# A hybrid recurrent layer on one core: a pinned pair of expansions, and column sums by products of 512 columns

## The chip, the core and the metric

The kernel runs on one core of a Trainium2 chip. TensorE multiplies matrices, VectorE, ScalarE and GpSimd work on tiles in SBUF, and each engine, with SyncE, can issue transfers on its queue. The metric is the time of one execution in device microseconds, the median over several runs.

## The reference

One layer of a streaming encoder is computed for a prompt of 512 frames and a sample of 64, with 2048 features, all in fp32:

```
mod = silu(c) @ w_ada + b_ada;  sh1, sc1, g1, sh2, sc2, g2 = split(mod, 6)
h = rmsnorm(x, norm1) * (1 + sc1) + sh1
proj = h @ w_in                     # gated linear attention (4 heads), gated delta rule (8 heads)
mix = concat(gla(...), gdn(...)) @ w_out
x = x + g1 * mix
h = rmsnorm(x, norm2) * (1 + sc2) + sh2
gate, val = split(h @ w_up, 2)
x = x + g2 * ((silu(conv3(gate) + b) * val) @ w_down)
y = rmsnorm(x, final_norm)
```

`c` is one vector for the prompt and one for the sample, `w_ada` is 2048 x 12288. The delta rule runs a causal convolution of width 4 on q, k and v, and solves, in every block of 64 frames, a unit lower triangular system:

```
lower = strict_tril(kb @ k.T * decay)
sol = triangular_solve(eye + lower, [v * beta, kb * exp(G)])
```

## The kernel before

Prompt and sample go through together, 576 columns as two halves of 288. Every large product is three fp32r products, since a weight tile is split into a high part on ScalarE (L651, `wh`) and a rest on VectorE (L652, `wl`): `hh,wh`, `hl,wh` and `hh,wl`, each for two halves, six matmuls for a step of 128 rows (`mm6`, L562 and L564). A weight tile holds 8 such steps, and `wh` and `wl` come from rings of three.

After the head come 54 column tiles of the input projection (`in_tile`, 16 steps each), then the output projection, the up and the down projection. Under the input projection run three streams, advanced a bit after each step by `tick`: the *jobs* (the recurrences, one per head, written as generators that yield and `rest` a number of ticks), `later` (a function that is to run so many ticks on), and *ada*, the modulation's remaining 16 blocks of 512 columns. The order in which instructions are then placed on an engine is chosen by the framework's scheduler from dependencies and priorities; each engine executes its list in order, so an instruction that waits holds all behind it.

*The inverse.* `inverse16` inverts the 16 x 16 diagonal blocks of a delta job. The matrices go to DRAM and come back with 32 blocks on 32 partitions (`d<-m`, `m<-d`), GpSimd works through 14 rows (L372 and L373), and the result goes to DRAM (L378) and comes back as `cm`, 128 partitions. After REST_X ticks, and 14 more (`FIRST_LATE`) in the first job, VectorE expands `cm` by a block mask into two tiles `m` of 512 columns (L387, twice). From them TensorE doubles the block size: L247, an eviction on VectorE (L1941), L254, and so on.

*The convolution.* `gdn_conv` copies a projected tile to `gcb`, and runs one product on ScalarE and three multiply-adds on VectorE (L1005).

*The modulation.* `ada_block` takes half-megabyte pieces of `w_ada` and accumulates them on VectorE, with one column of silu(c) as the scalar, into `acc` of 128 x 512 for prompt and sample (L833 starts, L835 goes on, 32 instructions a block). The sum over partitions is left: eight fp32 matmuls with `acc` as weights and a column of ones as the other side (L841) put 8 columns into PSUM, with the 512 outputs on partitions; the trace shows 16, since fp32 takes two passes. `put_mod` (L812) adds the bias from there.

Of the kernel before, what the change touches and what calls it, by code (L numbers as in the profile page):

```python
# [8 lines left out]
F32 = mybir.dt.float32  # L9
F32R = mybir.dt.float32r  # L10
I32 = mybir.dt.int32
AF = mybir.ActivationFunctionType
ALU = mybir.AluOpType
# [3 lines left out]
P = 128  # L17
# [18 lines left out]
REST_D, REST_X, REST_T, REST_N, REST_G = 8, 12, 6, 8, 4  # L36
# [8 lines left out]
FIRST_LATE = 14  # L45
# [58 lines left out]
class Kern:  # L104
# [67 lines left out]

        return cols.unsqueeze(2).to_broadcast([P, cols.shape[1], w])

    def gdn(self, qF, kF, x, gain, hcols, gb_src, s0, s_out, o_put, last_level, late=0):

# [4 lines left out]
        nc, c = self.nc, self.c  # L183
        V, A, T = self.jv, self.ja, nc.tensor
# [50 lines left out]
        u, t = yield from self.inverse16(a, gb, late)  # L235
# [5 lines left out]
        turn = lambda: None  # L241
        for s in (16, 32):
# [14 lines left out]
            if s < last_level:  # L257
                turn = lambda s=s: A.activation(half(t, s, 0), half(self.transpose4(u), s, 0), AF.Copy)
# [23 lines left out]
        for b in range(4):  # L282
# [12 lines left out]
            w = self.half()  # L295
# [54 lines left out]
    def inverse16(self, a, spare, late):  # L350

        nc, c, G = self.nc, self.c, self.nc.gpsimd
        pitch = 4 * P
        d0 = self.dp.tile([8 * (16 * pitch + 16)], F32, tag="d0", bufs=2, name=self.name("d0"))
        d1 = self.dp.tile([2, 32, 256], F32, tag="d1", bufs=2, name=self.name("d1"))
        G.dma_start(d0[:P * pitch].rearrange("(p f) -> p f", p=P), a.rearrange("p b t -> p (b t)"))
        lane = spare[:32].rearrange("p b t -> p (b t)").rearrange("p (w f) -> p w f", w=2)  # L360
        xx, xt = [lane[:, n].rearrange("p (i j) -> p i j", i=16) for n in range(2)]
        yield from self.rest(REST_S)
        blocks = d0.rearrange("(n f) -> n f", n=8)[:, :16 * pitch].rearrange("n (i b j) -> n i b j", i=16, b=4)
        for b in range(4):
            G.dma_start(xx[8 * b:8 * b + 8], blocks[:, :, b, :16])
        yield from self.rest(REST_D)
        G.memset(lane[:, 0, 0:256:17], 1.0)
        for i in range(1, 15):
            yield WAIT
            rest = slice(i + 1, 16)  # L370
            sh = [32, 15 - i, i]
            G.tensor_tensor(xt[:, rest, :i], xx[:, rest, i:i + 1].to_broadcast(sh), xx[:, i:i + 1, :i].to_broadcast(sh), op=ALU.mult)  # L372
            G.tensor_tensor(xx[:, rest, :i], xx[:, rest, :i], xt[:, rest, :i], op=ALU.add)  # L373
            yield WAIT
        yield from self.rest(REST_P)
        G.tensor_copy(xt, xx.rearrange("p i j -> p j i"))
        yield from self.rest(2)
        G.dma_start(d1.rearrange("w q f -> q w f"), lane)  # L378
        yield from self.rest(REST_S)
        cm = self.sp.tile([P, 2, 4, 16], F32, tag="cm", bufs=2, name=self.name("cm"))  # L380
        for w in range(2):
            G.dma_start(cm[:, w], d1[w].rearrange("(b n) (i j) -> (n i) b j", b=4, i=16))
        yield from self.rest(REST_X + late)
        sh = [P, 4, 8, 16]
        t, u = self.m4(), self.m4()
        for w, x in enumerate((t, u)):
            nc.vector.tensor_tensor(x.rearrange("p b (n j) -> p b n j", n=8), cm[:, w].unsqueeze(2).to_broadcast(sh),  # L387
                                    c["bd16"].rearrange("p (n j) -> p n j", n=8).unsqueeze(1).to_broadcast(sh), op=ALU.mult)
        yield from self.rest(HOP)
        return u, t  # L390

# [430 lines left out]
    def ada_block(self, blk, acc, raw):  # L822

        nc = self.nc
        V, T = nc.vector, nc.tensor
        acc = [a() for a in acc]
        for k0 in range(0, KD, 2):
            w = raw(blk, k0)
            for k in range(2):
                for s in range(2):  # L830
                    col = self.ct[:, s, k0 + k:k0 + k + 1]
                    if k0 + k == 0:
                        V.tensor_scalar_mul(acc[s], w[:, k], col)  # L833
                    else:
                        V.scalar_tensor_tensor(acc[s], w[:, k], col, acc[s], op0=ALU.mult, op1=ALU.add)  # L835
                    yield
        yield from self.rest(4)
        pc = self.bank()
        for j in range(4):
            for s in range(2):  # L840
                T.matmul(pc[:, 2 * j + s:2 * j + s + 1], acc[s][:, j * P:(j + 1) * P], self.c["ones"][:, 0:1],  # L841
                         start=True, stop=True)
        self.put_mod(blk // 4, 4 * (blk % 4), pc)

    def ada_raw(self, blk, k0):

# [147 lines left out]
    def gdn_conv(self, ps, t, dst, name, h):  # L994

        nc = self.nc
        V, A = nc.vector, nc.scalar
        cb = self.gcb
        acc = self.ap.tile([P, 582], F32, tag="ca", bufs=1, name=self.name("ca"))
        A.activation(cb[:, 3:515].rearrange("p (h t) -> p h t", h=2), ps[:, :, :HP], AF.Copy)  # L1000
        V.tensor_copy(cb[:, 518:582].rearrange("p (h t) -> p h t", h=2), ps[:, :, HP:HT])
        A.activation(cb[:, 515:518], self.vmap["st_conv"].rearrange("p (i t) -> p t i", i=3)[:, t], AF.Copy)
        A.activation(acc[:, :579], cb[:, 0:579], AF.Copy, scale=self.vec("gdn_conv_w", t))
        for j in range(1, 4):
            V.scalar_tensor_tensor(acc[:, :579], cb[:, j:j + 579], self.vec("gdn_conv_w", 24 * j + t), acc[:, :579],  # L1005
                                   op0=ALU.mult, op1=ALU.add)
        A.activation(dst, acc[:, 0:512], AF.Silu)
        A.activation(self.cs[:, 0, :, t], cb[:, 512:515], AF.Copy)
        A.activation(self.cs[:, 1, :, t], cb[:, 579:582], AF.Copy)
        self.put_s(name, h, lambda s: A.activation(s, acc[:, 515:579], AF.Silu))  # L1010
# [13 lines left out]
    def gdn_heads(self):  # L1024
        nc, o = self.nc, self.o
        A = nc.scalar
        b4 = lambda t: t.rearrange("p (b t) -> p b t", b=4)
        def conv_tile(n, off, h):
            ps = (self.ps_q0, self.ps_k0)[n] if h == 0 and n < 2 else self.in_tile(off + h * P)
            t = self.m("qkv")  # L1030
            self.gdn_conv(ps, 8 * n + h, t, "qkv"[n], h)
            return b4(t)

        def qk(h):
            q = conv_tile(0, OFF_BQ, h)
            if h == 0:
                self.narrow(self.kp)
            k, x = conv_tile(1, OFF_BK, h), {}
            self.jobs.append(self.gdn(q, k, x, self.vec("gdn_norm", 0), slice(4 * h, 4 * h + 4),
                                      self.gd[4 * h:4 * h + 4], None, o["p_gdn"][0, 0, h],  # L1040
                                      lambda t: self.put_o(8 + h, t), 64, FIRST_LATE if h == 0 else 0))
            return x

        def vg(h, x):
            v = conv_tile(2, OFF_BV, h)
            x["v"], x["at"] = lambda: v, self.ticks
            if h in GATES_BY:
                self.side = self.gla_gate(GATES_BY.index(h))
            ps = self.in_tile(OFF_BG + h * P)
            gt = self.m("gt")  # L1050
            A.activation(self.halves(gt), ps[:, :, :HP], AF.Silu)
            self.put_s("g", h, lambda t: A.activation(self.halves(t), ps[:, :, HP:HT], AF.Silu))
            x["gate"] = lambda: b4(gt)

        xs = [qk(0)]
        for h in range(8):
            if h < 7:
                xs.append(qk(h + 1))
            vg(h, xs[h])
        self.jobs.append(self.gdn_samples())  # L1060

        for s in range(2):
            ps = self.bank()
            nc.tensor.transpose(ps[:72, :P], self.cs[:, s].rearrange("p i t -> p (i t)"), self.c["ident"])
            rw = self.half()
            nc.vector.tensor_copy(rw[:72], ps[:72, :P])
            nc.sync.dma_start(o["ps"[s] + "_conv"][0, 0].rearrange("i (n p) -> i n p", p=P).rearrange("i n p -> (i n) p"), rw[:72])
# [778 lines left out]
def layer_kernel(tc, i, o):  # L1846
    nc = tc.nc
    with ExitStack() as ctx:
# [17 lines left out]
        with ExitStack() as early:  # L1866
            K.wp = pool(early, "wp", "right", bufs=3)
            with ExitStack() as right:
# [9 lines left out]
                with ExitStack() as st:  # L1878
# [3 lines left out]
                    K.jobs, K.due, K.ticks, K.at_job, K.at_ada = [], [], 0, 0.0, 0.0  # L1882
                    K.dp = dp
                    acc = [lambda n=n: K.ap.tile([P, 512], F32, tag=f"acc{n}", bufs=1, name=K.name("acc")) for n in range(2)]
                    K.ada = K.ada_blocks(range(8, 24), acc)
                    K.side = iter(())
                    K.gdn_heads()
# [10 lines left out]
                    K.drain()  # L1898
                    for _ in K.ada:
                        pass  # L1900
            K.sp = pool(ctx, "sp2", bufs=2)
            K.zp = pool(ctx, "zp", bufs=1)
            K.ua = pool(ctx, "ua", bufs=1)
# [99 lines left out]
```

## Time and profile before

| | |
|---|---|
| median of 3 runs | 2853.79 us (2853.17 to 2856.24) |
| the profiled execution | 2861.94 us, span 2860.2 us |
| mean granted TensorE clock | 0.987 |
| TensorE, VectorE, ScalarE, GpSimd busy | 2787.5, 2248.9, 1296.2, 317.9 us |
| the last L841 | begins at 1123.9 us |

Times inside the trace count from the start of the span. In a row of a timeline the brackets hold the idle time of the engine before that row and what ended it. In a row by window the engines stand in the order named in its head, then the granted clock, the DMA share and GB/s. Up to about 140 us is the head, the input projection runs to about 1085, the output projection to about 1310, the up projection to 2300, and the rest is the down projection and the end.

### The profile page before, as it was taken

The numbers are of one execution on the slowest core, as the hardware profiler recorded it, in microseconds if no ns is written. First come the engines' busy times: TensorE is split into PE (matmuls) and PEld (weight loads), VectorE is DVE, ScalarE is ACT, GpSimd is POOL, SyncE is SP. The second block draws the span as 40 slices with busy tenths as digits, with TensorE's granted clock in tenths as the row PEclk, the third lists the DMA queues.
The fourth block names the chain that finished last, engine by engine and source line by source line (L and its number), as shares of the span: only waits on it lengthen the run. The fifth ranks groups of instructions, "written<-read, shape, count | busy, mean of one in ns | idle before, by whom it ended". The sixth has DMA issues, their size and how long they took to land.

```text
span 2860.2 us, 51761 instructions
## 1 busy us (share of the span) xinstructions
PE 2787.5 (97%) x20560; PEld 2698.7 (94%) x20560; DVE 2248.9 (79%) x3728; ACT 1296.2 (45%) x2286; POOL 317.9 (11%) x597
## 2 busy tenths in 40 slices
PE   7898999999999999999999999999999999999998
PEld 3598999999999999999999999999999999999997
DVE  2477888777778787478887888888888889999996
ACT  4264556544433333255444444444444464444553
POOL 1023333224210001000000000000000000000000
PEclk9999999999999999999999999999999999999999
DMA  9964555545456448433333333333333343444461
GB/s 331 338 183 134 147 160 155 165 137 162 121 158 180 141 131 257 117 114 102 102 102 107 103 110 104 102 108 109 101 102 102 109 145 117 124 123 124 125 171 67
DMA packets 521984, 399.77 MB, mean 140 GB/s; under 512 B 50681, under 2 KB 453442, under 8 KB 521742
## 3 DMA queue, kind: packets, MB, share of 16 engines
q1 hardware_dynamic: 515966, 385.55, 45.6%
q0 software_dynamic: 5776, 10.91, 1.3%
q8 instruction: 162, 2.65, 0.4%
q14 instruction: 80, 0.66, 0.1%
HBM read 356.24 MB, written 40.13 MB: 139 GB/s over the span
## 4 chain that ended last, share of the span: by engine, by line
PE 79%; DVE 9%; issue 5%; DMA 4%; ACT 1%; POOL 1%; SPq 0%; ACTq 0%; DVEq 0%; POOLq 0%
PE g L562 19%; PE g L564 9%; PE g L1385 9%; PE g L1386 8%; PE g L1387 8%; PE bank L1386 3%; PE bank L1385 3%; PE bank L1387 3%; DVE wl L1570 2%; PE g L1618 2%; PE g L1620 2%; PE g L1619 2%; DMA raw<-in_w_down_dram 1%; DVE slot L1635 1%; PE bank L164 1%
## 5 line engine op out<-in xcount | busy, mean ns | idle before, releaser
L1385 PE MATMUL g<-slot,wh 128*128 128x290 f32 x1760 | 533.1, 303 | 2.7 <-ACT p L1397 2.7
L1386 PE MATMUL g<-slot,wh 128*128 128x290 f32 x1760 | 526.0, 299 | 0.0
L1387 PE MATMUL g<-slot,wl 128*128 128x290 f32 x1760 | 520.4, 296 | 0.0
L562 PE MATMUL g<-hh,wh 128*128 128x288 f32 x1984 | 450.1, 307 | 3.9 <-ACT wh L651 2.8
L564 PE MATMUL g<-hh,wl 128*128 128x288 f32 x1984 | 434.1, 299 | 3.5 <-DVE wl L652 3.4
L562 PE MATMUL g<-hl,wh 128*128 128x288 f32 x1984 | 432.2, 298 | 0.0
L1332 ACT ACTIVATE wh<-raw 128x1024 fp32r<-128x1024 f32 x176 | 187.1, 1063 | 392.5 <-PE g L1386 379.3
L1385 PEld LDWEIGHTS g<-slot,wh 128*128 128x128 f32 x1760 | 331.2, 188 | 16.7 <-ACT p L1397 11.7
L1387 PEld LDWEIGHTS g<-slot,wl 128*128 128x128 f32 x1760 | 336.1, 191 | 0.0
L1386 PEld LDWEIGHTS g<-slot,wh 128*128 128x128 f32 x1760 | 334.4, 190 | 0.1
L562 PEld LDWEIGHTS g<-hh,wh 128*128 128x128 f32 x1984 | 320.8, 191 | 7.7 <-ACT wh L651 3.1
L564 PEld LDWEIGHTS g<-hh,wl 128*128 128x128 f32 x1984 | 321.2, 190 | 4.2 <-DVE wl L652 4.0
L562 PEld LDWEIGHTS g<-hl,wh 128*128 128x128 f32 x1984 | 322.5, 190 | 0.1
L651 ACT ACTIVATE wh<-raw 128x1024 fp32r<-128x1024 f32 x147 | 155.7, 1061 | 287.8 <-PE g L562 262.0
L835 DVE SCALAR_TENSOR_TENSOR acc<-xr,ct,acc 128x512 f32<-128x512 f32 x322 | 231.4, 752 | 0.1
L1333 DVE TENSOR_TENSOR wl<-raw,wh 128x1024 fp32r<-128x1024 f32 x176 | 214.8, 1221 | 19.8 <-ACT wh L1332 19.7
L1618 PE MATMUL g<-slot,wh 128*128 128x288 f32 x760 | 224.4, 295 | 1.2 <-DVE slot L1635 1.2
L1620 PE MATMUL g<-slot,wl 128*128 128x288 f32 x760 | 223.9, 295 | 0.3 <-DVE wl L1570 0.3
L1619 PE MATMUL g<-slot,wh 128*128 128x288 f32 x760 | 224.2, 295 | 0.0
L652 DVE TENSOR_TENSOR wl<-raw,wh 128x1024 fp32r<-128x1024 f32 x147 | 180.0, 1225 | 49.3 <-ACT wh L651 47.8
L1386 PE MATMUL bank<-slot,wh 128*128 128x290 f32 x704 | 210.6, 299 | 0.0
L1385 PE MATMUL bank<-slot,wh 128*128 128x290 f32 x704 | 210.0, 298 | 0.0
(435 smaller groups left out, 5954.2 us busy)
## 6 DMA issues: line engine op xcount, KB each, us to landing
raw<-in_w_up_dram SPq DMA_DIRECT2D x176, 512.0 KB, 4.1
raw<-in_w_in_dram SPq DMA_DIRECT2D x108, 512.0 KB, 4.2
xr<-in_w_ada_dram SPq DMA_DIRECT2D x86, 512.0 KB, 3.8
raw<-in_w_down_dram SPq DMA_DIRECT2D x76, 512.0 KB, 3.6
ax<-in_w_ada_dram SPq DMA_DIRECT2D x42, 512.0 KB, 3.7
raw<-in_w_out_dram SPq DMA_DIRECT2D x32, 512.0 KB, 5.0
actd<-v SPq DMA_DIRECT2D x44, 256.0 KB, 4.5
hraw<-in_w_ada_dram SPq DMA_DIRECT2D x21, 512.0 KB, 8.8
```

Source lines behind the costliest of these rows:

```text
L562: T.matmul(ps[:, h if bank is None else bank, :n], wh, x[:, h, :n], start=f, stop=False)
L564: T.matmul(ps[:, h if bank is None else bank, :n], wl, ah[:, h, :n], start=False, stop=stop)
L652: nc.vector.tensor_tensor(lo[:, :n_], raw[:, :n_], hi[:, :n_].bitcast(F32), op=ALU.subtract)
L835: V.scalar_tensor_tensor(acc[s], w[:, k], col, acc[s], op0=ALU.mult, op1=ALU.add)
L1332: self.nc.scalar.activation(hi, src, AF.Copy)
L1333: self.nc.vector.tensor_tensor(lo, src, hi.bitcast(F32), op=ALU.subtract)
L1385: T.matmul(ps, wh[:, j], hi, start=(c < 3 and j == 0), stop=False, skip_group_check=True)
L1386: T.matmul(ps, wh[:, j], lo, start=False, stop=False, skip_group_check=True)
L1387: T.matmul(ps, wl[:, j], hi, start=False, stop=(j == NPAIR - 1), skip_group_check=True)
L1618: T.matmul(ps, wh[:, j, f], hi, start=(c < 3 and j == 0), stop=False, skip_group_check=True)
L1619: T.matmul(ps, wh[:, j, f], lo, start=False, stop=False, skip_group_check=True)
L1620: T.matmul(ps, wl[:, j, f], hi, start=False, stop=(j == n - 1), skip_group_check=True)
```

## The change

The expansions of the first job may be placed only behind the last convolution instruction that has been given out at that time; `issue_after` fixes an order on the engine and adds no semaphore. In the other jobs nothing is pinned. And the sums over partitions are made with `acc`, split into a high part and a rest, as the moving side, and 66 columns of ones and zeros as weights: rows 0 to 32 of the bank get the prompt's sums, 33 to 65 the sample's. Two rows are copied to SBUF, written to DRAM (`md`, two transfers on ScalarE's queue), read back six ticks later with outputs on partitions (`mc`, two transfers of 128 x 4 single elements), and added to the bias 16 ticks after that place (`put_mod`, now L813).

```diff
-        yield from self.rest(REST_X + late)
+        yield from self.rest(REST_X + (late or 0))
...
-        for w, x in enumerate((t, u)):
-            nc.vector.tensor_tensor(x.rearrange("p b (n j) -> p b n j", n=8), cm[:, w].unsqueeze(2).to_broadcast(sh),
-                                    c["bd16"].rearrange("p (n j) -> p n j", n=8).unsqueeze(1).to_broadcast(sh), op=ALU.mult)
+        with self.tc.issue_after(self.conv_of) if late is not None else ExitStack():
+            for w, x in enumerate((t, u)):
+                nc.vector.tensor_tensor(x.rearrange("p b (n j) -> p b n j", n=8), cm[:, w].unsqueeze(2).to_broadcast(sh),
+                                        c["bd16"].rearrange("p (n j) -> p n j", n=8).unsqueeze(1).to_broadcast(sh), op=ALU.mult)
...
+        A = nc.scalar
+        hi, lo = [self.wq.tile([P, 1024], F32R, tag="w" + c, bufs=3, name=self.name("w" + c))
+                  .rearrange("p (s n) -> p s n", s=2) for c in "hl"]
+        for s in range(2):
+            A.activation(hi[:, s], acc[s], AF.Copy)
+            V.tensor_tensor(lo[:, s], acc[s], hi[:, s].bitcast(F32), op=ALU.subtract)
+        yield from self.rest(3)
+        pc = self.bank()
+        for n, (x, s) in enumerate((x, s) for x in (hi, lo) for s in range(2)):
+            T.matmul(pc[:66], self.pick[:, 33 * s:33 * s + 66], x[:, s], start=(n == 0), stop=(n == 3))
+        rows = self.xr()[:, :512]
+        A.activation(rows[:66], pc[:66], AF.Copy)
+        md = self.dp.tile([2, 512], F32, tag="md", bufs=2, name=self.name("md"))
+        mc = self.ap.tile([P, 8], F32, tag="mc", bufs=1, name=self.name("mc"))
+        for s in range(2):
+            A.dma_start(md[s:s + 1], rows[33 * s:33 * s + 1])
+
+        def turn():
+            for s in range(2):
+                A.dma_start(mc[:, s:8:2], md[s].rearrange("(j p) -> p j", p=P))
+
+        self.later(6, turn)
+        self.later(16, lambda: self.put_mod(blk // 4, 4 * (blk % 4), mc))
         yield from self.rest(4)
-        pc = self.bank()
-        for j in range(4):
-            for s in range(2):
-                T.matmul(pc[:, 2 * j + s:2 * j + s + 1], acc[s][:, j * P:(j + 1) * P], self.c["ones"][:, 0:1],
-                         start=True, stop=True)
-        self.put_mod(blk // 4, 4 * (blk % 4), pc)
...
             V.scalar_tensor_tensor(acc[:, :579], cb[:, j:j + 579], self.vec("gdn_conv_w", 24 * j + t), acc[:, :579],
                                    op0=ALU.mult, op1=ALU.add)
+        self.conv_of = nc.cur_bb.bb.instructions[-1]
...
+                    K.pick = K.ap.tile([P, 99], F32R, name="pick")
+                    for n, f in enumerate((1.0, 0.0, 1.0)):
+                        nc.scalar.activation(K.pick[:, 33 * n:33 * n + 33], K.c["ones"][:, :33], AF.Copy, scale=f)
...
                     for _ in K.ada:
                         pass
+                    K.run_later(all=True)
```

`late` is now None by default and for every job but the first. A line of the new file stands one further down up to the modulation, 18 or 19 after it, and 23 for the recurrences' helper (L1941 becomes L1964). The following rows are the engines' lists as the two programs hold them.

VectorE before, at the first job's expansions; `s` and `rk` are small tiles of that job, `acc` the modulation's:

```order
255 L1941 TENSOR_TENSOR rk_2029<-nbe,s_291_1897 128x4
256 L387 TENSOR_TENSOR m_2502<-cm_2272,consts_1312 128x512
257 L1941 TENSOR_TENSOR s_291_1897<-nbeta,s_291_1897 128x4
258 L1941 TENSOR_TENSOR qkv_1583<-qkv_1583,m_1777 128x512
259 L1941 TENSOR_TENSOR m_1932<-bank_2094,m_1932 128x512
260 L387 TENSOR_TENSOR m_2503<-cm_2272,consts_1312 128x512
261 L1941 TENSOR_TENSOR m_1931<-bank_2093,m_1931 128x512
262 L812 TENSOR_TENSOR mod<-bank_2125,cols 128x8
263 L833 TENSOR_SCALAR acc_2135<-ax_1988,ct 128x512
```

VectorE now, where the expansions (L388) stand; L843 is the rest of `acc`:

```order
303 L1023 SCALAR_TENSOR_TENSOR ca_2457<-gcb,cols,ca_2457 128x579
304 L836 SCALAR_TENSOR_TENSOR acc_2192<-xr_2626,ct,acc_2192 128x512
305 L1023 SCALAR_TENSOR_TENSOR ca_2457<-gcb,cols,ca_2457 128x579 x2
306 L388 TENSOR_TENSOR m_2513<-cm_2281,consts_1312 128x512
307 L388 TENSOR_TENSOR m_2514<-cm_2281,consts_1312 128x512
308 L1964 TENSOR_TENSOR m_2596<-m_2485,cum 128x512
309 L843 TENSOR_TENSOR wl_2892<-acc_2191,wh_2891 128x512
310 L1964 TENSOR_TENSOR m_1441<-bank_2532,consts_1312 128x256
```

They moved from row 256, ahead of the second block's accumulations, to row 306 behind them; between rows 254 and 305 now lie 30 L836, 2 L834, 6 L653, 6 L1023, 2 L1019, one L813 and 6 small ones.

TensorE before, at the same job's first doubling (`m_2503` is an expansion):

```order
563 L564 MATMUL g_2461<-hh_869,wl_2464 128x288 x2
564 L247 MATMUL bank_2523<-m_2503,m_1571 128x64 x4
565 L562 MATMUL g_2461<-hh_894,wh_2463 128x288 x2
566 L562 MATMUL g_2461<-hl_895,wh_2463 128x288 x2
567 L564 MATMUL g_2461<-hh_894,wl_2464 128x288 x2
```

TensorE now:

```order
570 L565 MATMUL g_2470<-hh_1069,wl_2604 128x288 x2
571 L563 MATMUL g_2470<-hh_1094,wh_2603 128x288
572 L247 MATMUL bank_2532<-m_2514,m_1575 128x64 x4
573 L563 MATMUL g_2470<-hh_1094,wh_2603 128x288
574 L563 MATMUL g_2470<-hl_1095,wh_2603 128x288 x2
```

L247 moved from ahead of the tile's step `hh_894` into the step `hh_1094`, past the steps 894, 919, 1044 and 1069: 25 products of 288 columns on.

ScalarE now, in the third of the 16 blocks; `ca` is a gate of the linear attention, L857 the return of the sums, L652 a weight split:

```order
329 L1964 ACT_TABLE_LOAD
330 L1964 ACTIVATE ca_3766<-ca_3766,consts_95 128x512
331 L1964 ACTIVATE ca_3766<-ca_3766,consts_95 128x64
332 L857 DMA mc_3722<-md_3721 128x4x1 x2
333 L1020 ACTIVATE gcb<-cols 128x3
334 L1964 ACT_TABLE_LOAD
335 L1964 ACTIVATE m_4316<-m_4316 128x512
336 L652 ACTIVATE wh_4077<-raw_4076 128x1024
```

VectorE now, at the same block's modulation:

```order
489 L1964 TENSOR_TENSOR m_2485<-bank_3845,consts_1312 128x256
490 L1964 SCALAR_TENSOR_TENSOR ca_3766<-gcb,ca_3766 128x512
491 L1964 SCALAR_TENSOR_TENSOR ca_3766<-gcb,ca_3766 128x64
492 L1964 SCALAR_TENSOR_TENSOR gcb<-consts_95,ca_3766 128x128 x4
493 L813 TENSOR_TENSOR mod<-mc_3722,cols 128x8
494 L653 TENSOR_TENSOR wl_4078<-raw_4076,wh_4077 128x1024
```

L813 stands six instructions behind the gate that ScalarE finishes just ahead of L857; behind it waits the rest of a weight tile. The eight L841 of each block have gone from TensorE's list, and four L847 (`bank<-wh,pick` and `bank<-wl,pick`, 66x512) stand in it instead.

More of the change, by code (lines that the diff above doesn't have):

```diff
@@ L173, in col4, with gdn @@
         return cols.unsqueeze(2).to_broadcast([P, cols.shape[1], w])
-    def gdn(self, qF, kF, x, gain, hcols, gb_src, s0, s_out, o_put, last_level, late=0):
+    def gdn(self, qF, kF, x, gain, hcols, gb_src, s0, s_out, o_put, last_level, late=None):
         nc, c = self.nc, self.c
@@ L1040, in qk @@
                                       self.gd[4 * h:4 * h + 4], None, o["p_gdn"][0, 0, h],
-                                      lambda t: self.put_o(8 + h, t), 64, FIRST_LATE if h == 0 else 0))
+                                      lambda t: self.put_o(8 + h, t), 64, FIRST_LATE if h == 0 else None))
             return x
```

## The prediction

> **What bounds the kernel now.** I read the page's totals first, then busy time by stretch, then the one stretch that stands out.
>
> ```profile
> span 2860.2 us, 51761 instructions
> PE 2787.5 (97%) x20560; PEld 2698.7 (94%) x20560; DVE 2248.9 (79%) x3728; ACT 1296.2 (45%) x2286; POOL 317.9 (11%) x597
> core 0: us, PE busy (x) PEld busy (x) DVE busy (x) ACT busy (x) POOL busy (x), PEclk, DMA share, GB/s
> 200.00:310.00 110.00, 97.12 (x717) 92.94 (x716) 78.01 (x160) 48.36 (x119) 56.20 (x101) 0.94 0.46 128
> 310.00:1000.00 690.00, 688.86 (x5254) 673.19 (x5253) 541.06 (x1122) 315.30 (x736) 153.89 (x274) 0.99 0.53 154
> 1000.00:1100.00 100.00, 97.28 (x705) 92.77 (x704) 82.98 (x192) 38.59 (x72) 6.81 (x25) 0.97 0.54 155
> ```
>
> TensorE is the bound: from 310 to 1000 us it idles 1.1 us in 690, so there a microsecond taken from TensorE is a microsecond off the end, and work on VectorE (541 of 690 busy) or ScalarE (315) is free until it makes TensorE wait. From 200 to 310 us TensorE idles 12.9 us. What it idles for shows in VectorE's timeline:
>
> ```profile
> 204.35 0.16 DVE L1941 TENSOR_TENSOR rk<-nbe,s 128x4 f32<-128x4 f32 x1
> 217.78 0.69 DVE L387 TENSOR_TENSOR m<-cm,consts 128x512 f32<-128x512 f32 x1 [13.27 <-DMA cm<-d]
> 223.05 1.41 DVE L835 SCALAR_TENSOR_TENSOR acc<-xr,ct,acc 128x512 f32<-128x512 f32 x2
> 224.38 1.22 DVE L652 TENSOR_TENSOR wl<-raw,wh 128x1024 fp32r<-128x1024 f32 x1
> 238.87 0.86 DVE L1005 SCALAR_TENSOR_TENSOR ca<-gcb,cols,ca 128x579 f32<-128x579 f32 x1
> ```
>
> L387 stands at VectorE's head for 13.27 us and waits for the small inverse to come back through DRAM; the weight splits (L652) that TensorE needs are queued behind it. TensorE's own timeline, then its busy time and granted clock (the number before the DMA share):
>
> ```profile
> 221.46 0.54 PE L562 MATMUL g<-hh,wh 128*128 128x288 f32 x2 [2.85 <-ACT wh L651]
> 225.66 0.85 PE L564 MATMUL g<-hh,wl 128*128 128x288 f32 x2 [3.40 <-DVE wl L652]
> 244.85 1.00 PE L247 MATMUL bank<-m,m 128*128 128x64 f32 x8
> 252.39 1.97 PE L254 MATMUL bank<-m,m 128*128 128x64 f32 x8 [5.15 <-DVE m L1941]
> 216.00:220.00 4.00, 2.61 (x20) 2.38 (x18) 2.21 (x5) 1.42 (x5) 0.00 (x0) 1.00 0.07 9
> 220.00:225.00 5.00, 0.80 (x4) 0.57 (x4) 5.00 (x10) 3.99 (x7) 1.71 (x3) 0.84 0.31 78
> 225.00:230.00 5.00, 4.34 (x18) 4.35 (x19) 5.00 (x8) 0.00 (x0) 1.50 (x5) 0.50 0.91 264
> 245.00:250.00 5.00, 2.24 (x19) 2.01 (x17) 5.00 (x9) 1.41 (x3) 4.50 (x7) 1.00 0.86 251
> 250.00:255.00 5.00, 2.61 (x12) 2.61 (x13) 3.70 (x7) 2.57 (x5) 2.87 (x4) 0.57 0.53 152
> 255.00:260.00 5.00, 5.00 (x34) 5.00 (x34) 1.62 (x2) 0.91 (x5) 1.55 (x2) 0.75 0.70 183
> ```
>
> Idle in these rows is 1.39 + 4.20 + 0.66 + 2.76 + 2.39 = 11.4 us. Busy time at a lowered clock is lost too: 4.34 x 0.50 + 2.61 x 0.43 + 5.00 x 0.25 + 0.80 x 0.16 = 4.7 us. The stall, and the backlog behind it (the 5.15 us wait at 252), cost **16 us**.
>
> **Part one, the pin.** The two L387 instructions move from VectorE's row 256 to behind the convolution. What VectorE now runs in between, from 204.5 us: 30 accumulations (1.41/2, less overlap 0.67 each, 20.1 us), 2 starts (0.9), 6 splits (1.15 pitch, 6.9), 6 convolution steps (0.76, 4.6), and about 2.4 us of small ones: 34.9 us, to 239.4. One L813 lies among them (part two; I give it 2.7 us), and the expansions take 1.2: done at about 243.3.
>
> The late transfer `cm` is hidden: GpSimd's steps towards it slow down when VectorE is not idle,
>
> ```profile
> 203.46 0.27 POOL L373 TENSOR_TENSOR m<-m 32x44 f32<-32x44 f32 x1
> 234.75 0.71 POOL L372 TENSOR_TENSOR m<-m 32x44 f32<-32x44 f32 x1
> ```
>
> and the steps still left at 204.5 took 6.2 us; at up to 0.71/0.27 they take 16, so `cm` lands by about 228, with 13 us in hand.
>
> What is late next is TensorE's L247, which reads the expansions. It came at 244.85; without the two waits (6.25) and the half clock after them (2.2) that place is reached at 236.4. The change puts it 25 products of 288 columns later (0.134 each, row 286.72 below: 3.3), so TensorE arrives at about 239.5 and waits **about 4 us**. Another 1 us goes at L254, whose eviction stands three instructions behind the expansions on VectorE, and 2 us at a lower clock, as after the 5.15 us wait (1.1 + 1.25). Left of the 16: **9 us**. The ends: 16 if nothing waits; 3, if both later waits are twice as long and the clock drops in full.
>
> On the 2 us of clock there is also a rule: the Trainium skill ("TensorE: Matmul & The Clock Gate", Part 1) has the clock halved after an idle window of about 3.4 us that runs freely; by it a 4 us wait may or may not fill a window, and the term is 0 or 2. The row at 250 us agrees, with 5.15 us idle and 0.57 behind it.
>
> **Part two, the sums.** The old products, by source, in the chain and in place:
>
> ```profile
> L841 PE MATMUL bank<-consts,acc x256: 164/250/307, 203.9 to 1123.9; 128*128 128x1 f32 x128
> 341.63 1.68 PE bank L841 x16
> 284.62 1.90 PE L841 MATMUL bank<-consts,acc 128*128 128x1 f32 x16
> 286.72 0.43 PE L564 MATMUL g<-hh,wl 128*128 128x288 f32 x2
> 286.99 0.43 PE L562 MATMUL g<-hh,wh 128*128 128x288 f32 x2
> ```
>
> Sixteen blocks of 16 products with one column cost 1.68 us each. The four new ones are fp32r products like L562: pairs of 288 columns start 0.27 apart, so 0.134 each, and 512 columns 0.237; four take 0.95 us. Saved: 0.73 x 16 = **11.7 us** of TensorE. Were the 66 columns of weights no cheaper to load and the fill exposed (0.3, the difference between a product's duration and its pitch), 1.25 and 6.9 us.
>
> What is added, per block:
>
> ```profile
> L1000 ACT ACTIVATE gcb<-g 128x512 f32<-128x512 f32 x23 | 13.7, 596 | 3.1 <-PE g L564 3.1
> L387 DVE TENSOR_TENSOR m<-cm,consts 128x512 f32<-128x512 f32 x18 | 12.2, 688 | 13.9 <-DMA cm<-d 13.3 <-PE bank L294 0.6
> L365 POOL DMA_DIRECT2D m<-d x36 | 21.9, 614 | 23.1 <-DMA d<-m 17.9 <-DVE s L1941 2.8 <-DVE acc L835 2.4
> d<-m POOLq DMA_DIRECT2D x9, 64.0 KB, 2.0
> cm<-d POOLq DMA_DIRECT2D x18, 32.0 KB, 3.5
> ```
>
> VectorE: two subtractions, 1.4 us. ScalarE: three activations, 1.8 us, and four DMA issues on its own queue; no row shows ScalarE issuing one, so by GpSimd's 0.61 at most 2.5 us, and about 2.0 us in which the return waits for the row written out (as `d<-m`). Over 16 blocks that is 22 us on VectorE and at most 100 on ScalarE, against 149 and 375 us free from 310 to 1000. The splits queued behind the waiting ScalarE have one weight tile as cover: 8 x 6 products of 0.134, 6.4 us. The three pick activations precede the narrow phase and are lost in ScalarE's free time.
>
> The price that can hurt is L813. Before, the modulation read PSUM; now VectorE waits at its head until `mc` has come, 512 single elements. `cm<-d`, 512 pieces of 16, lands in 3.5 us. In the third block the return is issued as ScalarE finishes the gate's last activation, and on VectorE six instructions of the gate (some 1.6 us) stand between that activation and L813; so VectorE stands 3.5 + 0.8 - 1.6 = 2.7 us. Does such a stand cost TensorE? The same place has stood before, as long:
>
> ```profile
> 343.13 0.49 DVE L833 TENSOR_SCALAR acc<-xr,ct 128x512 f32<-128x512 f32 x1 [4.21 <-PE bank L841]
> 944.63 0.49 DVE L833 TENSOR_SCALAR acc<-ax,ct 128x512 f32<-128x512 f32 x1 [3.98 <-PE bank L841]
>   DVE acc L833: 22.4, 7
>   DVE mod L812: 8.8, 8
> ```
>
> VectorE waited 22.4 + 8.8 = 31 us for L841, up to 4.2 us at a time, and TensorE stayed full. Those waits go, since the accumulators are now released by the copies; 16 x 2.7 = 43 us come. I charge TensorE 0.2 us a block for it, 3 us, and 1 us for the first block, where the products follow the subtractions at once: **4 us**, bounds 0 and 12 (0.7 a block, all that the products save).
>
> The stream of blocks also ends later: its last old product stands at 1123.9, and by the order of the new program the last new ones stand at a place that was reached at 1178, with L813 at about 1184.
>
> ```profile
> 1100.00:1200.00 100.00, 98.90 (x745) 98.67 (x744) 51.34 (x78) 24.29 (x29) 4.26 (x6) 1.00 0.66 187
> L1173 DVE TENSOR_TENSOR slot<-xr,slot x4: 757/758/760, 1135.9 to 1143.1; 128x576 fp32r<-128x576 f32 x4
> ```
>
> VectorE and ScalarE are half and three quarters idle there, so the accumulations are hidden. What moves with them are four of the eight conversions of the mixers' outputs for the second half of the output projection (L1173, in the new file L1192): done by 1144 before, now behind the last block, so that all eight, 6 us, follow 1184.5. The first product that reads them stood at about 1202. I cost this at 0; were the 11 us of cover gone, it costs the length of the last L813's stand, 3 us, inside the bounds of the 4.
>
> Against `mc` speaks the Trainium skill ("DMA: Bandwidth & Descriptors", Rules for kernel authors): a last dimension that is not contiguous becomes one descriptor per element. By it `mc` has 512 descriptors, as many as `cm` has pieces, and the 3.5 us would stand; no row here has 4-byte pieces alone.
>
> **Sum.** 9 + 11.7 - 4 = 17 us off. Against the profiled execution's own 2861.9 that is 2845; its time lies 8.1 over the median 2853.8, so the median comes to **2837 us**.
>
> **Rivals.** *The stands eat the sums' gain* (0.2). For it: splits lose one of three slots in each ring while hi and lo are held. Against it: the 31 us above cost nothing. Then 11.7 goes and 9 less some 2 remains: 2847, range 2841 to 2853.
>
> *Everything is hidden* (0.1): TensorE is not late at L247 because VectorE's rows run faster than I add them, and no stand counts: 16 + 11.7 = 28 off, 2826. Against it: VectorE is 100% busy in these rows.
>
> *The wait only moves* (0.05): expansions at 243 hold TensorE, at half clock, as long as L387 did, and the sums give back all but a little: within 3 us of 2854.
>
> *Slower, by `mc`* (0.15): its pieces queue behind half-megabyte weight loads. The slowest small load has
>
> ```profile
> fr<-in_w_in_dram SPq DMA_DIRECT2D x8, 256.0 KB, 9.8
> ```
>
> and if `mc` takes 9.8, VectorE stands 9.8 - 1.6 = 8.2 us at each L813, 1.8 us beyond the cover of one tile: 16 x 1.8 = 29 lost against 21 won, 8 slower, 2862. It decides from a stand of 6.4 + 21/16 = 7.7 us. For it: the DMA share is 0.53 throughout; against: `cm` meets the same traffic and lands in 3.5.
>
> **Numbers.** The forecast has 0.5, with its own range 2830 to 2843 (terms 9 and 4 between 5 and 12, 0 and 7). A measurement of this kernel tells 0.2%, 5.7 us, from nothing: faster means under 2848, slower over 2859.5. Faster: 0.5 + 0.1 + half of the first rival, 0.70. Same: its other half and 0.05, 0.15. Slower 0.15. The range leaves out the slower case: 2825 to 2858.
>
> **What would show it.** VectorE's 13.27 us gap gone, L388 near 242 and a TensorE wait of 3 to 5 us there at L247; the windows 216 to 235 at clock 1.00; L847 four to a block in about 0.95 us; L813 waiting 1 to 4 us on DMA `mc`; TensorE still idle under 5 us from 310 to 1000, that stretch's work ending some 11 us sooner. I am wrong if TensorE shows waits for `wl` or `wh` behind each L813 or L857, or if L247's wait exceeds 9 us.

## The result, and the profile after

The changed kernel takes 2839.02 us (median of 4 runs, 2832.49 to 2840.33) against 2855.01 of the kernel before beside it: a ratio of 0.9936, 95% interval 0.9918 to 0.9954. It is faster by 16 us, where 17 were forecast; timed again with five runs it took 2837.35 us against 2858.03, a ratio of 0.9930 (0.9918 to 0.9941). The profiled execution after took 2832.49 us, span 2830.7.

Busy time by stretch of the kernel after, in the columns known from before (PE, PEld, DVE, ACT, POOL, clock, DMA share, GB/s):

```profile
200.00:310.00 110.00, 103.93 (x778) 98.92 (x776) 91.67 (x186) 56.81 (x141) 58.28 (x95) 0.98 0.56 159
310.00:1000.00 690.00, 684.85 (x5180) 663.33 (x5179) 541.66 (x1112) 328.73 (x756) 158.36 (x266) 1.00 0.52 151
1000.00:1100.00 100.00, 96.50 (x704) 92.51 (x704) 84.54 (x199) 37.75 (x73) 11.05 (x31) 0.98 0.63 183
1100.00:1200.00 100.00, 100.00 (x748) 99.35 (x747) 66.90 (x102) 31.50 (x45) 0.56 (x3) 1.00 0.65 183
241.00:245.00 4.00, 3.97 (x20) 3.97 (x21) 2.79 (x5) 1.42 (x2) 3.29 (x10) 0.57 0.04 8
```

From 200 to 310 us TensorE idles 6.1 us, where it idled 12.9. From 310 to 1000 it idles 5.2 us, where it idled 1.1 and the prediction named under 5: the change brought new waits there. From 1100 to 1200, where the blocks' stream now ends, it is never idle.

Rows of the timelines of VectorE and TensorE after, at the first job's expansions and the first block's bias, and the new products by source:

```profile
213.86 0.17 DVE L813 TENSOR_TENSOR mod<-mc,cols 128x8 f32<-128x8 f32 x1 [3.15 <-DMA mc<-md]
239.50 1.48 DVE L388 TENSOR_TENSOR m<-cm,consts 128x512 f32<-128x512 f32 x2
241.03 1.60 PE L247 MATMUL bank<-m,m 128*128 128x64 f32 x8 [4.79 <-DVE m L388]
244.46 1.20 PE L254 MATMUL bank<-m,m 128*128 128x64 f32 x8
L847 PE MATMUL bank<-wh,pick x32: 387/397/478, 199.8 to 1151.3; 128*66 128x512 f32 x32
L847 PE MATMUL bank<-wl,pick x32: 389/395/472, 200.3 to 1151.8; 128*66 128x512 f32 x32
```

The 13.27 us gap is gone, and what is left of the stall is one wait of 4.79 us at L247 and a clock of 0.57 over the four microseconds behind it.

Both programs hold the same 18,072 products of 128 x 128 weights with 288 or 290 columns, so the start of the n-th of them, counted from 0, can be compared between traces. This table is worked out from the traces in that way; the second column is the second profile of the kernel before, the others are differences from it in us:

| n | before (2nd), us | before (1st) | pin only | sums only | after (1st) | after (2nd) | no return |
|---|---|---|---|---|---|---|---|
| 576 | 207.5 | -1.9 | -1.1 | -3.7 | -5.1 | -3.5 | -3.2 |
| 960 | 295.0 | +0.3 | -13.4 | -4.2 | -11.7 | -9.6 | -10.2 |
| 2304 | 536.8 | +0.3 | -10.8 | -8.2 | -17.2 | -15.8 | -17.7 |
| 4992 | 1013.3 | +1.9 | -10.9 | -12.4 | -23.5 | -21.5 | -26.6 |
| 6912 | 1300.2 | +3.7 | -11.4 | -10.2 | -22.8 | -19.9 | -27.1 |
| 18048 | 2835.0 | +6.7 | -9.7 | -9.6 | -22.7 | -18.2 | -24.5 |

Between 207 and 295 us the pin acts; from there to 1013 us the sums bring a little at each block; behind that single executions differ by some us either way.

### The profile page after: what moved, and what is told of

The parts are those of the page before. It is cut to its first block, busy times and chain, and to the rows that moved or that the text cites. A ratio compares the mean times of both kernels' runs of the same rounds, so it can differ in the third digit from the quotient of the medians.

```text
span 2830.7 us, 51579 instructions
## 1 busy us (share of the span) xinstructions
PE 2766.1 (98%) x20368; PEld 2671.2 (94%) x20368; DVE 2271.7 (80%) x3760; ACT 1312.7 (46%) x2330; POOL 334.8 (12%) x597
## 4 chain that ended last, share of the span: by engine, by line
PE 76%; DVE 8%; DMA 3%; ACT 2%; issue 1%; SPq 0%; ACTq 0%; POOL 0%; DVEq 0%
PE g L563 17%; PE g L1404 9%; PE g L1405 8%; PE g L1406 8%; PE g L565 8%; PE bank L1405 3%; PE bank L1404 3%; PE bank L1406 3%; PE g L1639 2%; PE g L1637 2%; PE g L1638 2%; DVE wl L1589 2%; DMA mc<-md 1%; DVE acc L836 1%; PE bank L164 1%
## 5 line engine op out<-in xcount | busy, mean ns | idle before, releaser
L652 ACT ACTIVATE wh<-raw 128x1024 fp32r<-128x1024 f32 x147 | 155.8, 1060 | 239.5 <-PE g L563 181.0
L836 DVE SCALAR_TENSOR_TENSOR acc<-xr,ct,acc 128x512 f32<-128x512 f32 x322 | 229.5, 749 | 10.4 <-DMA xr<-in_w_ada_dram 10.4
L653 DVE TENSOR_TENSOR wl<-raw,wh 128x1024 fp32r<-128x1024 f32 x147 | 179.6, 1222 | 47.2 <-ACT wh L652 44.6
```

The source lines that it names most:

```text
L653: nc.vector.tensor_tensor(lo[:, :n_], raw[:, :n_], hi[:, :n_].bitcast(F32), op=ALU.subtract)
```

## The experiments

### The two parts apart

The pin alone is the changed kernel with the old end of `ada_block`; the sums alone is it without the pin:

```diff
-        with self.tc.issue_after(self.conv_of) if late is not None else ExitStack():
+        with ExitStack():
```

The changed kernel itself ran beside them.

> The changed kernel itself, timed again beside its two halves. Theory (the two parts act in different stretches and add up): 14 to 18 us under the kernel before, 0.9937 to 0.995 of its time, and in the new profile again one wait of 4 to 6 us at L247 and about 0.8 us a block from 300 to 1000 us. Rival (the 29 us between the two traces are the true size and the medians are chance): 25 us or more under.

> The pin alone; the sums over partitions are the old products of one column. Theory: the stretch from 200 to 300 us gives about 9 us, nothing after it changes: 8 to 10 us under the kernel before. Rival (the wait only moves to L247 and the backlog costs the same): within 3 us of the kernel before. Rival (the pin also needs the freed place of the old products): under 5 us.

> The products of 512 columns with the return through DRAM alone; the first job's expansions are not pinned and stand early on VectorE again. Theory: 13.27 us of VectorE standing for cm are back, the later blocks bring 0.73 us each less a few us of stands: 6 to 10 us under the kernel before. Rival (the return costs what the products save): within 3 us of it. Rival (the sums bring most, since each block also frees VectorE from waiting for the old products): 13 us or more under.

Measured, against 2858.03 us: both 2837.35 (0.9930, 0.9918 to 0.9941), the pin 2846.45 (0.9959, 0.9947 to 0.9971), the sums 2844.44 (0.9951, 0.9938 to 0.9964). For both, 14 to 18 us and a wait of 4 to 6 us at L247 were expected; it came to 20.7 us, and in this second profile the wait is 3.78 us. The pin alone is worth 11.6 us, a little over the forecast 8 to 10, and in the table it comes in one step and stays. The sums alone are worth 13.6, past the expected 6 to 10 and in the rival's range; what the rival says, that freeing VectorE from waiting for the old products brings it, is not shown by that. TensorE's waits with the pin alone (first row) and with the sums alone (the other two):

```profile
240.88 1.10 PE L247 MATMUL bank<-m,m 128*128 128x64 f32 x8 [1.29 <-DVE m L388]
214.40 0.53 PE L565 MATMUL g<-hh,wl 128*128 128x288 f32 x2 [3.58 <-DVE wl L653]
246.52 1.95 PE L254 MATMUL bank<-m,m 128*128 128x64 f32 x8 [4.79 <-DVE m L1964]
```

Without the pin the stall is back at its two places. With the pin alone TensorE waits 1.29 us at L247 and not 4.79: it comes later, since the blocks' old products stand before it, and VectorE's expansions come as soon. So a part of what the first blocks' sums save is spent at that wait, some 3 us. The parts' gains add up to 25.2 us and both bring 20.7; the intervals are wide enough that this difference alone would not show it.

### The pin one convolution sooner

```diff
-        self.conv_of = nc.cur_bb.bb.instructions[-1]
+        self.conv_pre, self.conv_of = getattr(self, 'conv_of', None), nc.cur_bb.bb.instructions[-1]
...
-        with self.tc.issue_after(self.conv_of) if late is not None else ExitStack():
+        with self.tc.issue_after(self.conv_pre) if late is not None else ExitStack():
```

> Both parts, but the expansions pinned behind the convolution before the last one given out: row 291 of VectorE in place of 306, some 12 us sooner, when cm has been there for some 8 us. Theory (the 4.8 us wait at L247 and the clock behind it are what is left of the stall): 3 to 6 us under the changed kernel. Rival (TensorE's order moves too, L247 comes sooner, and the eviction ahead of L254 then stands behind accumulations as before the change): no faster than the changed kernel, or slower by up to 5 us, with the wait at L254.

Measured: 2837.44 us (0.9929, 0.9917 to 0.9940), the same as the changed kernel. The rival holds. VectorE's rows, then TensorE's:

```profile
231.16 1.29 DVE L388 TENSOR_TENSOR m<-cm,consts 128x512 f32<-128x512 f32 x2
241.20 0.41 DVE L1964 TENSOR_TENSOR m<-bank,consts 128x256 f32<-128x256 f32 x1
236.36 1.00 PE L247 MATMUL bank<-m,m 128*128 128x64 f32 x8
241.67 1.10 PE L254 MATMUL bank<-m,m 128*128 128x64 f32 x8 [3.18 <-DVE m L1964]
```

The expansions come 8 us sooner and L247 no longer waits, but its eviction then stands on VectorE behind eight accumulations, a split, a copy and two convolution steps, until 241.20, and L254 waits 3.18 us for it. So VectorE's full list limits this place more than the point of the pin does.

### A product's price

```diff
-        for n, (x, s) in enumerate((x, s) for x in (hi, lo) for s in range(2)):
-            T.matmul(pc[:66], self.pick[:, 33 * s:33 * s + 66], x[:, s], start=(n == 0), stop=(n == 3))
+        for r in range(3):
+            for n, (x, s) in enumerate((x, s) for x in (hi, lo) for s in range(2)):
+                T.matmul(pc[:66], self.pick[:, 33 * s:33 * s + 66], x[:, s], start=(n == 0), stop=(n == 3))
```

> The changed kernel with its four products made three times over in each block, the same sums written again each time: 8 more products of 512 columns a block, 128 in all. Theory (from 300 us on TensorE sets the end, a product costs 0.23 us there): 128 x 0.23 = 30 us over the changed kernel. Rival (TensorE has slack at the blocks' ends): under 15 us over it.

Measured: 2863.41 us (1.0027, 1.0018 to 1.0036, of 2855.74), 24 to 26 us over the changed kernel's two medians: 0.19 to 0.20 us for each of 128 products, of the 0.23 us that one takes on TensorE. Most of a product's time arrives at the end, so the saving at the blocks' ends counts too: in the two first traces the old products take 1.70 us from their first start to the next product's, the new ones 0.93, so 0.77 x 16 = 12.3 us of TensorE's time.

The old products seem to cost more than their own time. Two stretches of the first profile before, then the same two after:

```profile
580.00:590.00 10.00, 10.00 (x72) 9.54 (x72) 7.74 (x15) 2.72 (x6) 7.17 (x15) 0.83 0.25 68
760.00:770.00 10.00, 10.00 (x58) 10.00 (x57) 5.83 (x13) 3.46 (x5) 0.00 (x0) 0.66 0.25 61
580.00:590.00 10.00, 10.00 (x80) 10.00 (x80) 5.39 (x15) 4.84 (x18) 2.12 (x3) 1.00 0.36 101
760.00:770.00 10.00, 10.00 (x69) 9.56 (x69) 9.34 (x20) 5.08 (x11) 0.00 (x0) 1.00 0.70 213
```

TensorE has no gap in any of them, and yet its clock is lowered before. In the three traces with the old products (before twice, the pin alone) it falls to half seven times between 310 and 1100 us, each time within 2 us behind the end of a block's sixteen, for 3.4 or 6.8 us; half of these times, 8.5, 3.4 and 3.4 us in the three traces, is lost. In the changed kernel's two traces and in that without the return it falls there only at a wait of some 2 us or more. Why two or three blocks of sixteen have such a fall and the others none is not shown.

### When the bias is added

Two kernels add it 26 ticks on and not 16; the second also orders the first block's behind the accumulations given out by then:

```diff
+                    self.acc_of = nc.cur_bb.bb.instructions[-1]
...
-        self.later(16, lambda: self.put_mod(blk // 4, 4 * (blk % 4), mc))
+        def bias():
+            with self.tc.issue_after(self.acc_of) if blk == 8 else ExitStack():
+                self.put_mod(blk // 4, 4 * (blk % 4), mc)
+
+        self.later(26, bias)
```

> The changed kernel with the bias added 26 ticks after the return's place and not 16: L813 stands two to ten rows later on VectorE in most blocks, in the first block where it was. Theory (after the first block VectorE's stands for mc are under TensorE's backlog and cost nothing): the waits for mc fall from 16 to 18 us to under 8, the time stays within 3 us of the changed kernel. Rival (TensorE pays for each stand): 8 us or more under it.

> As the one before, and the first block's bias is ordered behind the accumulations given out by then, six of them, 4 us later. Theory (the first block's stand of 2.8 to 3.2 us lies ahead of the first job's expansions, so L247 waits for it in full): the wait at L247 falls from 3.8 to 4.8 us to under 2, 2 to 4 us under the kernel with the late bias alone. Rival (the freed time is taken by the accumulations, or the wait moves to L254): within 1.5 us of it.

Measured, against 2855.74: 2838.00 (0.9936, 0.9924 to 0.9949) and 2835.55 us (0.9931, 0.9917 to 0.9944). The waits for `mc` fell from 15.7 us to 8.3 and 6.1 and the time did not clearly move: the 2.4 us between the two lie inside the spread of their executions. The wait at L247, expected under 2 us in the second, stayed. VectorE and TensorE in the second kernel:

```profile
215.03 0.75 DVE L836 SCALAR_TENSOR_TENSOR acc<-xr,ct,acc 128x512 f32<-128x512 f32 x1 [2.79 <-DMA xr<-in_w_ada_dram]
242.18 1.97 PE L247 MATMUL bank<-m,m 128*128 128x64 f32 x8 [4.05 <-DVE m L388]
```

At the place where the bias had stood, the accumulation behind it now stands 2.79 us for its weights, as long as the bias stands for `mc` in the kernel with the late bias alone (2.73). The stand hid another one.

### Without the return

```diff
-        md = self.dp.tile([2, 512], F32, tag="md", bufs=2, name=self.name("md"))
-        mc = self.ap.tile([P, 8], F32, tag="mc", bufs=1, name=self.name("mc"))
-        for s in range(2):
-            A.dma_start(md[s:s + 1], rows[33 * s:33 * s + 1])
...
-        self.later(6, turn)
-        self.later(16, lambda: self.put_mod(blk // 4, 4 * (blk % 4), mc))
+        self.later(16, lambda: self.put_mod(blk // 4, 4 * (blk % 4), self.c["ones"]))
```

> The changed kernel without the return: the products and the copy of the bank stay, the four small transfers of a block are left out, and the bias is added to a constant tile, so that the sums do not reach the modulation of blocks 8 to 23 (that part of the computation is left out). Theory (VectorE's stands for mc cost TensorE nothing but the chain from the one at 987 us through SyncE's queue to the wait at 1003): 1 to 4 us under the changed kernel, and the wait for qkv at 1003 falls from 1.7 to 3.3 us to about 1.4, as before the change. Rival (TensorE pays for the stands, 16 to 18 us in all): 8 us or more under. Rival (nothing is paid): within 1 us.

Measured: 2828.75 us against 2858.11 (0.9899, 0.9885 to 0.9912), 8 to 10 us under the changed kernel, whose interval it does not touch. The theory's 1 to 4 us fell; the return costs more than was charged for it. VectorE's waits in the changed kernel's first profile, then, without the return, its waits and TensorE at L247:

```profile
DVE mod L813 <- DMA mc<-md: 15.7, 9, 4.2
DVE acc L836 <- DMA xr<-in_w_ada_dram: 10.4, 9, 3.0
DVE acc L836 <- DMA xr<-in_w_ada_dram: 6.2, 5, 2.4
239.98 1.92 PE L247 MATMUL bank<-m,m 128*128 128x64 f32 x8 [2.79 <-DVE m L388]
```

Without the return TensorE has no wait of half a microsecond left at 689, 812 and 1070 us, and shorter ones at L247 and 1003; one of 2.28 us at 1045 is new. Where stands come through is seen in the chain of waits of the changed kernel's second profile. First the one at 668, then the one at 987 (start, length, what):

```profile
663.80 4.38 DMA mc<-md
668.27 0.18 DVE mod L813
668.48 2.08 DVE acc L836 x3
670.56 1.20 DVE m L388 x2
...
688.85 0.34 DVE m L1964
689.24 0.77 PE bank L254 x5
980.44 6.80 DMA mc<-md
...
994.00 0.37 SPq L868
994.41 0.46 SPq L1003
994.92 3.98 DMA sd_ak<-ts
998.99 4.37 DMA qkv<-sd_ak
1003.40 1.22 PE bank L432 x4
```

VectorE stands for `mc` until 668.2, has no gap in the 20 us after, and hands the delay on to TensorE's L254, which waits 1.25 us at 689.24. And `mc` of 980.44 holds the accumulations, these hold a weights buffer, SyncE's next weights load (L868) waits for that buffer, and the transfers of the samples' keys behind it on SyncE's queue come late for L432, which waits 3.27 us.

### The bias in the next block

```diff
                         V.scalar_tensor_tensor(acc[s], w[:, k], col, acc[s], op0=ALU.mult, op1=ALU.add)
+                    if k0 == 10 and self.bias:
+                        with self.tc.issue_after(nc.cur_bb.bb.instructions[-1]):
+                            self.bias.pop()()
                     yield
...
-        self.later(16, lambda: self.put_mod(blk // 4, 4 * (blk % 4), mc))
+        self.bias.append(lambda: self.put_mod(blk // 4, 4 * (blk % 4), mc))
+        if blk == 23:
+            self.later(16, self.bias.pop())
...
-        self.n_ada = 0
+        self.n_ada, self.bias = 0, []
```

> The changed kernel, with the bias of each block ordered behind the next block's tenth to twelfth accumulation, some 25 us into that block, so that mc has landed by then; the return through DRAM stays. Theory (the 8 us that leaving out the return gave are VectorE's stands, carried along its full list to the waits at 689, 812 and 1003): VectorE's waits for mc fall from 16 to 18 us to under 2, TensorE's waits at 689 and 812 to under 0.6 and the one at 1003 to about 1.2, 4 to 8 us under the changed kernel (0.990 to 0.9915 of the kernel before). Rival (the 8 us are the transfers' issue on ScalarE and their traffic): within 2 us of the changed kernel.

Measured: 2836.09 us against 2857.83 (0.9923, 0.9909 to 0.9938), 1.3 to 2.9 us under the changed kernel's two medians, about as the rival said. VectorE's waits and TensorE's timeline there:

```profile
DVE mod L813 <- DMA mc<-md: 0.4, 1, 0.4
DVE acc L836 <- DMA xr<-in_w_ada_dram: 18.6, 15, 2.8
808.59 0.33 PE L164 MATMUL bank<-consts,m 128*128 128x128 f32 x1 [0.24 <-ACT m L1969]
998.00 0.71 PE L432 MATMUL bank<-qkv,qkv 128*128 128x128 f32 x4 [2.01 <-DMA qkv<-sd_ak]
```

The stands for `mc` are gone, and TensorE's waits at 689 and 812 nearly so (the latter was 1.46); the one at 1003 is 2.01 us, where about 1.2 was expected. But the accumulations now wait 18.6 us for weights, where they waited 10.4. VectorE's stands for `mc` and for weights together fell only from 26.1 us to 19.0; with the late bias they are 20.5 and 20.7, without the return 6.2. So moving the bias mostly exchanged one stand for another, and this experiment does not tell what the stands are worth. Whether the longer waits for weights come from the two rows' buffer, which the transfers hold from the same ring as the weights, or from ScalarE's issues, was not tried and stays open.

### Blocks of 36 steps

```diff
-        yield from self.rest(4)
+        yield from self.rest(1)
```

> The changed kernel with one step of rest at the end of a block and not four: 36 steps a block, as before the change, so that the stream of blocks ends about 60 us sooner and meets other work at each place. Theory (what the blocks' ends meet is chance; the products save the same): within 3 us of the changed kernel. Rival (the waits of TensorE between 1000 and 1100 us, 6 to 7 us, come from the stream that runs on there): 3 to 5 us under it.

Measured: 2837.51 us against 2858.11 (0.9919, 0.9904 to 0.9935), 2837.35 in the changed kernel: the length of a block did not matter here. TensorE still waits 1.80 us at L500 near 1079 though the stream ends sooner, so that wait does not come from its running on.

### The return on GpSimd's queue

```diff
-            A.dma_start(md[s:s + 1], rows[33 * s:33 * s + 1])
+            nc.gpsimd.dma_start(md[s:s + 1], rows[33 * s:33 * s + 1])
...
-                A.dma_start(mc[:, s:8:2], md[s].rearrange("(j p) -> p j", p=P))
+                nc.gpsimd.dma_start(mc[:, s:8:2], md[s].rearrange("(j p) -> p j", p=P))
```

> The changed kernel with the four small transfers of a block issued on GpSimd's queue and not on ScalarE's. Theory (ScalarE's blocking for them is under TensorE's backlog): within 3 us of the changed kernel. Rival (the waits of TensorE for ScalarE at 595 and 812 us come from the blocked queue): those waits go and it is 2 to 4 us under. Rival (GpSimd's queue holds the inverse's transfers, and they come later behind the new ones): 3 to 8 us over, with longer waits for cm.

Measured: 2886.64 us against 2855.74 (1.0109, 1.0095 to 1.0123): 48 us over the changed kernel, far past the rival's 3 to 8, and slower than before the change. VectorE's waits for `mc`, two of them, TensorE's waits behind them, and the transfers' median time to landing:

```profile
DVE mod L813 <- DMA mc<-md: 59.8, 14, 12.4
224.67 0.17 DVE L813 TENSOR_TENSOR mod<-mc,cols 128x8 f32<-128x8 f32 x1 [12.40 <-DMA mc<-md]
316.05 0.17 DVE L813 TENSOR_TENSOR mod<-mc,cols 128x8 f32<-128x8 f32 x1 [12.18 <-DMA mc<-md]
252.43 1.97 PE L247 MATMUL bank<-m,m 128*128 128x64 f32 x8 [10.67 <-DVE m L388]
316.53 0.80 PE L294 MATMUL bank<-sq,m 128*128 128x128 f32 x2 [11.59 <-DVE sq L1964]
cm<-d POOLq DMA_DIRECT2D x18, 32.0 KB, 2.3
mc<-md POOLq DMA_DIRECT2D x32, 2.0 KB, 4.8
```

This is the prediction's slower rival, reached by another cause than its own: the transfer itself lands in 4.8 us, so it was its place on GpSimd's queue that made `mc` late, not weight loads. Nor was it `cm`, as this run's own rival had it: VectorE has no wait for `cm` there. Stands of 12 us, beyond the cover of one weight tile, went to TensorE nearly whole in these two places.

### The kernel before, looked at again

> The kernel before, a second profile of it. Theory (the first profiled execution was a long one of its kind, 8 us over its median, and the first of the changed kernel a short one, which makes 29 us of 16 to 20): the stretch of 200 to 310 us again idles 11 to 13 us on TensorE at the same two places, and the time is 2853 to 2862. Rival (the profiled executions are typical, and the stall is longer in them than in the others): the stretch idles the same, and the time is again about 2862.

Measured: 2855.20 us, span 2853.4. In this second profile of it:

```profile
200.00:310.00 110.00, 99.63 (x734) 95.46 (x733) 79.67 (x166) 48.31 (x119) 56.51 (x103) 0.94 0.45 129
225.18 0.85 PE L564 MATMUL g<-hh,wl 128*128 128x288 f32 x2 [3.55 <-DVE wl L652]
251.92 0.47 PE L254 MATMUL bank<-m,m 128*128 128x64 f32 x1 [5.01 <-DVE m L1941]
```

TensorE idles 10.4 us, a little under the 11 to 13 expected, at the same places. The first profile of before was 6.7 us longer, and by the table it lost that after 537 us, not at the stall; there its lowered clock behind the old products cost 8.5 us and not 3.4. Two traces can therefore differ by 29 us where the medians differ by 16 to 21.

## Why the prediction was right

The forecast of 2837 us stands at 2 us from the first measurement and at none from the second. The pin and the sums came out near their terms or above, the return was charged too little, and these errors cancel: that the number is so close is in part luck. The medians alone do not show it, since 11.6 for the pin and 12.3 for the products less 8 to 10 for the return make 14 to 16 us, where 16 to 21 were measured. The traces add up better. This table is worked out from them, from the 576th product to the 6912th; "clock" is TensorE's busy time multiplied by the share of the clock that was not granted, "work" is what is left:

| us | time | idle | clock | work |
|---|---|---|---|---|
| before (2nd) | 1092.7 | 16.4 | 8.6 | 1067.7 |
| pin only | 1082.4 | 10.7 | 3.4 | 1068.3 |
| sums only | 1086.2 | 21.4 | 8.1 | 1056.8 |
| after (1st) | 1075.0 | 14.7 | 3.4 | 1056.8 |
| after (2nd) | 1076.2 | 14.8 | 4.8 | 1056.6 |
| no return | 1068.9 | 8.2 | 5.1 | 1055.5 |

The pin takes 10 to 11 us of idle time and clock, with the sums and without. The new products take 11 us of work with the return and 12 to 13 without it. The return costs 6 to 7 us, nearly all of it TensorE's idle time. Together that is about 16 us of the 16.5 to 17.7 that the table shows.

*The pin, forecast 9 us.* Alone it brought 11.6 by the medians. That the wait at L247 was 4.79 us where 4 were worked out is partly luck, since both engines came to the place sooner. The rows that I added up began at 200.50 on VectorE and not at 204.5, and took 1.7 us longer, the first stand being 3.15 and not 2.7; the expansions were done at 240.98 and not 243.3. TensorE was 3.2 us ahead at the 576th product already and reached L247 at 236.2 and not 239.5. The 1 us at L254 did not come, and the lowered clock cost 3.97 x 0.43 = 1.7 us, where 2 were charged. The Trainium skill ("TensorE: Matmul & The Clock Gate", Part 1) gives an idle window of about 3.4 us; the trace agrees here, with 4.79 us idle and a clock of 0.57 behind it. The falls behind the old products came without idle time.

*The sums, forecast 11.7 us.* The products saved 12.3 us of TensorE's time; the row of fp32r products with 288 columns was the right one. What the old ones cost through the clock was not in the sum.

*The return, forecast 4 us, measured 8 to 10 by the medians and 6 to 7 in the traces.* This is the step that failed: "I charge TensorE 0.2 us a block". I argued from stands of VectorE for L841 that had cost nothing. The stands for `mc` were shorter than forecast (15.7 us in all and not 43) and yet cost, because VectorE's list behind some of them has no gap up to the next place where TensorE waits for it, and one reached SyncE's queue. The waits for weights, 10.4 us in place of 0.7, were in no term. The time to landing was wrong as well: `mc` took 4.4 to 6.8 us in the chain, and 4.8 against 2.3 for `cm` on one queue, where I had taken `cm`'s 3.5. The Trainium skill's rule ("DMA: Bandwidth & Descriptors", Rules for kernel authors), one descriptor per element, was no reason for 3.5 to stand: equal numbers of pieces did not make equal times.

*The late end of the blocks, forecast 0.* From 1100 to 1200 TensorE was full, so this held.

*The rivals.* "The stands eat the sums' gain" was half right: they and the return's other cost took 6 to 10 of 12.3 us. "The wait only moves" was true of its smaller part: one wait of 4.8 us in place of three of 11.4. "Everything is hidden" fell with it. The slower rival needed stands of 7.7 us; on ScalarE's queue the longest was 4.2.

## What to carry to other kernels

Pinning an instruction behind work that needs nothing from a slow round trip takes the whole stall from an engine's head, but the consumer then waits for the list it was put behind; moving the pin forward only moved the wait. A stand of an engine that is 80% busy is not free: follow its list to the next place where the bounding engine waits, and count the gaps on the way. And price a small transfer by one with the same size of pieces, not the same number.

## What was not expected of the hardware

Behind sixteen products of one column TensorE's clock fell to half for 3.4 us or more with no idle time in the trace, seven times in three traces; in the changed kernel's two traces it never fell there without a wait. A transfer of 512 single fp32 elements landed in 4.8 us (median of 32) on the queue on which one of 512 runs of 16 elements landed in 2.3 (18). And a chain of three engines' queues carried one late 2 KB transfer 16 us on to TensorE.
